# Windowed attention with fp16 copies of fp32 inputs: transposing q and k as 4-byte words, scores from every second fp16, value products grouped by shared weights

## The chip, the cores and the metric

The kernel runs on one core of one Trainium2 chip. Times are device microseconds (us) of an execution, given as medians over executions. All executions quoted here were fast: none was over 1.5% above the fastest of its kernel.

## The reference

Attention inside windows of 64 rows, over 4 x 4096 rows of 1536 numbers:

```python
B, S, D, W = 4, 4096, 1536, 64
logits = np.einsum('bnwd,bnud->bnwu', q_w, k_w) * D ** -0.5
logits = logits - logits.max(axis=-1, keepdims=True)
attn = np.exp(logits); attn = attn / attn.sum(axis=-1, keepdims=True)
out = np.einsum('bnwu,bnud->bnwd', attn, v_w)      # float32 in, float32 out
```

Three inputs of 100.66 MB are read and one output of 100.66 MB is written, so 402.6 MB must cross between HBM and the core, whatever the compute does.

## The kernel before

Work is cut into 32 units of 512 rows. A unit's q, k and v are loaded by GpSimd's software queue, which turns fp32 into fp16 on the way. q and k must be transposed, so that the 1536 columns lie across the partitions. TensorE does that into PSUM, and VectorE (DVE) and ScalarE (ACT) copy the result to SBUF. Score products, the exponential and the value products follow, and the evictions scale by the reciprocal of the row sum. The last unit is cut into three parts to shorten the end.

```python
DC = D // P                       # 12 chunks of 128 columns
tp_ps = ... bufs=3 ...            # PSUM banks for transposes
lt_ps = ... bufs=2 ...            # scores
o_ps  = ... bufs=2 ...            # outputs
s_ps  = ... bufs=1 ...            # row sums
# ... cut ...
def transpose(src, xt, c0, copy):
    tp = tp_ps.tile([P, CG * R, H, P], FP16, tag="tp", name="tp")       # CG = 2 in a full unit
    for c in range(c0, c0 + CG):
        for r in range(R):
            for j in range(H):
                nc.tensor.transpose(tp[:, (c - c0) * R + r, j, :],
                                    src[:, lo + R * j + r, c * P : (c + 1) * P], ident)
    dst = xt[:, c0 : c0 + CG, :].rearrange("p c (r e j) -> p (c r) j e", r=R, j=H)
    copy(out=dst, in_=tp)
# ... cut: product() accumulates the scores; all of q is transposed first, then
#     k group by group, each group followed by the product of the group before it ...
def values(u, i, h, et, last):
    # ... cut: all row sums, then one reciprocal ...
    for t in range(R):
        for j in range(NJ):
            o = o_ps.tile([P, 512], FP32, tag="o", name="o")
            for r in range(R):
                nc.tensor.matmul(o, lhsT=et[:, r, t, :], rhs=u.v[:, lo + R * h + r, sl],
                                 start=(r == 0), stop=(r == R - 1))
            # scaled eviction, in turn on ACT and DVE
# ... cut ...
for ui, u in enumerate(units):
    for i in range(len(u.parts)):
        blocks = scores(u, i)
        if i == 0:
            load_all(ui + 2, "qk")          # q and k have two buffers
        for h, et in blocks:
            values(u, i, h, et, last)
        if not last:
            store(u, i)
    load_all(ui + 3, "v")                   # v has three
```

The softmax here doesn't subtract the row's maximum and nothing guards it: scores larger than these inputs give would overflow.

Of the kernel before, what the change touches and what calls it, by code (L numbers as in the profile page):

```python
# [7 lines left out]
FP16 = mybir.dt.float16  # L8
FP32 = mybir.dt.float32

P = 128
W = 64
EXP = mybir.ActivationFunctionType.Exp
COPY = mybir.ActivationFunctionType.Copy
# [18 lines left out]
def kernel(  # L33
# [6 lines left out]
):  # L40
    nc = tc.nc
    B, S, D = q.shape
    DC = D // P
    NJ = D // 512
    scale = float(D) ** -0.5

# [6 lines left out]
    consts = ctx.enter_context(tc.tile_pool(name="consts", bufs=1))  # L53
    qkp = ctx.enter_context(tc.tile_pool(name="qkp", bufs=2))
    vp = ctx.enter_context(tc.tile_pool(name="vp", bufs=3))
    xtp = ctx.enter_context(tc.tile_pool(name="xtp", bufs=1))
    outp = ctx.enter_context(tc.tile_pool(name="outp", bufs=3))
    rsp = ctx.enter_context(tc.tile_pool(name="rsp", bufs=4))
    tp_ps = ctx.enter_context(tc.tile_pool(name="tp_ps", bufs=3, space=bass.MemoryType.PSUM))
    lt_ps = ctx.enter_context(tc.tile_pool(name="lt_ps", bufs=2, space=bass.MemoryType.PSUM))  # L60
    o_ps = ctx.enter_context(tc.tile_pool(name="o_ps", bufs=2, space=bass.MemoryType.PSUM))
    s_ps = ctx.enter_context(tc.tile_pool(name="s_ps", bufs=1, space=bass.MemoryType.PSUM))

    ctx.enter_context(tc.manual_schedule())
# [17 lines left out]
    def load_all(ui, names):  # L82
# [8 lines left out]
    nc.sync.dma_start(out=slots(raw, 0, SLOTS, SLOTS), in_=rows(qf, 0, SLOTS, SLOTS))  # L91
    load_all(0, "kv")

    ident = consts.tile([P, P], FP16, name="ident")
    ones = consts.tile([P, 8], FP16, name="ones")
    zeros = consts.tile([P, 1], FP32, name="zeros")
    nc.vector.memset(ident, 0.0)
# [3 lines left out]
        out=ident,  # L101
        in_=ident,
# [13 lines left out]
    for R in (2, 1):  # L116
        ets[R] = []
        for i in range(2):
            et = consts.tile([P, R, R, P], FP16, name=f"et{R}{i}")
# [5 lines left out]
    def scores(u, i):  # L125


        lo, hi, R = u.parts[i]
        n = hi - lo
        H = n // R  # L130
        CG = {4: 2, 2: 4, 1: 6}[n]
        xq = xtp.tile([P, DC, n * P], FP16, tag="xq", name="xq")
        xk = xtp.tile([P, DC, n * P], FP16, tag="xk", name="xk")
        lts = []
        for h in range(H):
            lt = lt_ps.tile([P, 512], FP32, tag="lt", name="lt")
            lts.append(lt[:, : R * R * P].rearrange("p (r s e) -> p r s e", r=R, s=R))

        def transpose(src, xt, c0, copy):

            tp = tp_ps.tile([P, CG * R, H, P], FP16, tag="tp", name="tp")
            for c in range(c0, c0 + CG):
                for r in range(R):
                    for j in range(H):
                        nc.tensor.transpose(  # L145
                            tp[:, (c - c0) * R + r, j, :],
                            src[:, lo + R * j + r, c * P : (c + 1) * P],
                            ident,
                        )
            dst = xt[:, c0 : c0 + CG, :].rearrange("p c (r e j) -> p (c r) j e", r=R, j=H)  # L150
            copy(out=dst, in_=tp)  # L151

        def product(c0, h):
            for c in range(c0, c0 + CG):
                kc = xk[:, c, :].rearrange("p (r h e) -> p r h e", r=R, h=H)
                qc = xq[:, c, :].rearrange("p (r h e) -> p r h e", r=R, h=H)
                for r in range(R):
                    nc.tensor.matmul(  # L158
                        lts[h][:, r, :, :],
                        lhsT=kc[:, r, h, :],  # L160
                        rhs=qc[:, :, h, :],
                        start=(c == 0 and r == 0),
                        stop=(c == DC - 1),
                        skip_group_check=True,
                    )

        starts = list(range(0, DC, CG))
        for c0 in starts:
            flip[0] += 1
            transpose(getattr(u, "q"), xq, c0, nc.scalar.copy if flip[0] % 3 == 0 else nc.vector.tensor_copy)  # L170
        for g, c0 in enumerate(starts):
            transpose(getattr(u, "k"), xk, c0, nc.scalar.copy if g % 2 == 1 else nc.vector.tensor_copy)
            if g > 0:
                for h in range(H):
                    product(starts[g - 1], h)
        blocks = []
        for h in range(H):
            product(starts[-1], h)
            et = ets[R][turn[R] % 2]
            turn[R] += 1  # L180
            w = W // R
            for a in range(0, P, w):
                s = slice(a, a + w)
                nc.scalar.activation(  # L184
                    et[s, :, :, s], lts[h][s, :, :, s], EXP, bias=zeros[s], scale=scale
                )
            blocks.append((h, et))
        return blocks

    def values(u, i, h, et, last):  # L190
        lo, hi, R = u.parts[i]
        if not hasattr(u, "o"):
            u.o = outp.tile([P, SLOTS, D], FP32, tag="out_sb", name="out_sb")
        sp = s_ps.tile([P, R, 2], FP32, tag="sp", name="sp")
        for t in range(R):
            for r in range(R):
                nc.tensor.matmul(  # L197
                    sp[:, t, 0:1], lhsT=et[:, r, t, :], rhs=ones[:, 0:1],
                    start=(r == 0), stop=(r == R - 1),
                )  # L200
        rs = rsp.tile([P, R], FP32, tag="rs", name="rs")
        nc.vector.reciprocal(out=rs, in_=sp[:, :, 0])  # L202
        n = 0
        for t in range(R):
            for j in range(NJ):
                o = o_ps.tile([P, 512], FP32, tag="o", name="o")
                sl = slice(512 * j, 512 * (j + 1))
                for r in range(R):
                    nc.tensor.matmul(  # L209
                        o, lhsT=et[:, r, t, :], rhs=u.v[:, lo + R * h + r, sl],  # L210
                        start=(r == 0), stop=(r == R - 1),
                    )
                dst = u.o[:, lo + R * h + t, sl]
                if n % 2 == 0:
                    nc.scalar.activation(dst, o, COPY, bias=0.0, scale=rs[:, t : t + 1])  # L215
                else:
                    nc.vector.tensor_scalar_mul(dst, o, scalar1=rs[:, t : t + 1])  # L217
                n += 1
                if last:
                    nc.sync.dma_start(out=of[u.first[i] : u.first[i] + P, sl], in_=dst)  # L220
# [5 lines left out]
    for ui, u in enumerate(units):  # L226
        for i in range(len(u.parts)):
            last = ui == N - 1 and i == len(u.parts) - 1
            blocks = scores(u, i)
            if i == 0:  # L230
                load_all(ui + 2, "qk")
# [4 lines that stand above are left out]
        load_all(ui + 3, "v")  # L236
# [30 lines left out]
```

## Time and profile before

| | before |
|---|---|
| time | 950.44 us, median of 3 (949.48 to 950.64) |
| traffic | 402.6 MB, 424 GB/s |
| distance between units in mid-run | 29.5 us |
| TensorE waiting for k in a unit | 2.8 us on average (78.4 us in 28 waits) |

First, lines of the page of the kernel before: the span; busy time of each engine with its instructions; the DMA row (busy tenths of the 16 DMA engines in each of 40 slices); the packet time of the main queue as a share of 16 engines' span; the HBM traffic.

```profile
span 948.6 us, 12985 instructions
...
PE 666.8 (70%) x5624; PEld 443.1 (47%) x5624; DVE 426.9 (45%) x491; ACT 434.2 (46%) x612; POOL 83.7 (9%) x139
...
DMA  9999999999999999999999999999999999999997
...
q0 software_dynamic: 27232, 249.31, 100.2%
...
HBM read 301.99 MB, written 100.66 MB: 424 GB/s over the span
```

The DMA row reads 9 in 39 of 40 slices, while the busiest engine, TensorE, is busy for 70%. "HBM Reference" of the Trainium skill, under Specifications (TRN2), gives about 425 GB/s for a core that streams alone; this trace has 424. (The prediction below names the section Access; the figure stands under Specifications.)

Next, groups of instructions of the same page: line, engine, operation, shapes, count | busy us, mean ns of one | idle time before them and what ended most of it.

```profile
...
L209 PE MATMUL o<-v,et 128*128 128x512 f16 x762 | 226.8, 402 | 65.6 <-ACT out_sb L215 61.4
L158 PE MATMUL lt<-xq,xk 128*128 128x256 f16 (+1 forms) x1536 | 236.9, 306 | 41.4 <-DVE xk L151 25.9
L151 ACT COPY xk<-tp 128x1024 f16<-128x1024 f16 (+1 forms) x96 | 123.6, 1287 | 255.8 <-PE tp L145 255.8
...
L151 DVE COPY xk<-tp 128x1024 f16<-128x1024 f16 (+1 forms) x97 | 123.3, 1271 | 200.7 <-PE tp L145 200.7
...
L145 PE MATMUL tp<-ident,k 128*128 128x128 f16 x1536 | 136.4, 245 | 81.7 <-DMA k<-in_k_dram 78.4
...
L209 PEld LDWEIGHTS <-et 128*128 128x128 f16 x762 | 72.7, 99 | 188.1 <-issue 147.5
...
L145 PE MATMUL tp<-ident,q 128*128 128x128 f16 x1536 | 103.0, 220 | 46.6 <-DVE xq L151 20.8
```

A PSUM copy takes 1.27 to 1.29 us. The value products (L209) have as many weight loads as matmuls. A transpose's mean of 220 or 245 ns is how long one takes from its start to its end. In a burst they overlap, and the timeline gives the real rate.

The waits view of the kernel before: who waited for whom, us in total, number of waits, longest.

```profile
...
PE tp L145 <- DMA k<-in_k_dram: 78.4, 28, 4.3
...
PE tp L145 <- DMA q<-in_q_dram: 3.2, 4, 1.4
```

And TensorE's timeline over one unit (start us, length us, what, count [idle before, releaser]):

```profile
...
330.54 1.50 PE L145 MATMUL tp<-ident,q 128*128 128x128 f16 x24
...
337.20 1.07 PE L145 MATMUL tp<-ident,k 128*128 128x128 f16 x16 [2.67 <-DMA k<-in_k_dram]
339.27 1.89 PE L158 MATMUL lt<-xq,xk 128*128 128x256 f16 x8 [1.01 <-DVE xk L151]
...
346.87 0.61 PE L145 MATMUL tp<-ident,k 128*128 128x128 f16 x8
347.55 1.05 PE L158 MATMUL lt<-xq,xk 128*128 128x256 f16 x8
...
359.99 1.50 PE L145 MATMUL tp<-ident,q 128*128 128x128 f16 x24
```

This unit starts at 330.54 and the next at 359.99. The q transposes come first, then a wait of 2.67 us for k. Eight k transposes take 0.61 us later on, which is 77 ns each with the latency of the burst counted in. 24 q transposes take 1.50 us. Eight score matmuls take 1.05 us at the end of the stage. "TensorE: Matmul & The Clock Gate" of the Trainium skill (Part 1) describes a clock that falls to half when the engine has been idle. This trace agrees: here is the stretch behind the wait (us; busy us of PE, PEld, DVE, ACT, POOL; granted clock; DMA share; GB/s), with a granted clock of 0.50.

```profile
...
338.20:344.95 6.75, 5.74 (x37) 4.58 (x36) 2.32 (x2) 1.63 (x2) 0.00 (x0) 0.50 1.02 293
```

The 16 transposes right behind the wait still ran at the full rate (1.07 us); the clock fell a microsecond later.

Last, the end of the run, in stretches of the trace (us; busy us of each engine; granted clock; DMA share; GB/s):

```profile
...
930.00:935.00 5.00, 4.34 (x39) 2.56 (x38) 2.89 (x5) 1.53 (x3) 0.55 (x1) 0.79 0.79 337
935.00:940.00 5.00, 3.13 (x40) 2.14 (x37) 1.94 (x4) 3.03 (x6) 0.55 (x1) 1.00 0.82 347
940.00:949.00 9.00, 1.51 (x10) 0.57 (x10) 0.92 (x2) 2.45 (x5) 0.00 (x0) 0.82 0.49 193
```

### The profile page before, as it was taken

Reading aid. Unit: us, or ns where it says so; the run is one execution under the profiler, and the core shown is the slowest. Engines: PE = TensorE matmul, PEld = TensorE weight load, DVE = VectorE, ACT = ScalarE, POOL = GpSimd, SP = SyncE. Lnnn points to the kernel's source line nnn. Section 1 sums busy time; section 2 is a strip of 40 time slices with the busy share of each in tenths; the row PEclk is TensorE's granted clock in tenths of the full one; section 3 lists DMA queues with packets and bytes.
Section 4 is the critical chain, followed back from the end, with each engine's and each line's share of the span. In section 5 each row is a group of like instructions: output and inputs, shape, how many; then the busy total and the mean of one; then the engine's idle time right before and its main releaser. Section 6 shows DMA issues by size and latency. Waiting matters only on the chain. (4 is left out here: it accounts for less than half of the span.)

```text
span 948.6 us, 12985 instructions
## 1 busy us (share of the span) xinstructions
PE 666.8 (70%) x5624; PEld 443.1 (47%) x5624; DVE 426.9 (45%) x491; ACT 434.2 (46%) x612; POOL 83.7 (9%) x139
## 2 busy tenths in 40 slices
PE   2777776776767867767667677776776767777685
PEld 1544554444544545445454354544445534455452
DVE  3545445443454344543445443454434545344442
ACT  2555434444345444454534454435544445453444
POOL 1101110100101011010010100101101001011010
PEclk9999989888899889798988998989988999798798
DMA  9999999999999999999999999999999999999997
GB/s 259 215 234 262 282 280 280 247 253 279 281 278 252 246 282 282 279 263 242 278 281 279 271 241 271 282 279 275 242 263 282 281 277 253 254 279 281 279 258 312
DMA packets 27865, 254.07 MB, mean 268 GB/s; under 512 B 2208, under 2 KB 2208, under 8 KB 11808
## 3 DMA queue, kind: packets, MB, share of 16 engines
q0 software_dynamic: 27232, 249.31, 100.2%
q1 hardware_dynamic: 576, 3.93, 1.1%
q8 instruction: 44, 0.72, 0.3%
q14 instruction: 13, 0.11, 0.0%
HBM read 301.99 MB, written 100.66 MB: 424 GB/s over the span
## 5 line engine op out<-in xcount | busy, mean ns | idle before, releaser
L209 PE MATMUL o<-v,et 128*128 128x512 f16 x762 | 226.8, 402 | 65.6 <-ACT out_sb L215 61.4
L158 PE MATMUL lt<-xq,xk 128*128 128x256 f16 (+1 forms) x1536 | 236.9, 306 | 41.4 <-DVE xk L151 25.9
L151 ACT COPY xk<-tp 128x1024 f16<-128x1024 f16 (+1 forms) x96 | 123.6, 1287 | 255.8 <-PE tp L145 255.8
L217 DVE TENSOR_SCALAR out_sb<-o,rs 128x512 f32<-128x512 f32 x191 | 143.4, 751 | 161.7 <-PE o L209 161.7
L151 DVE COPY xk<-tp 128x1024 f16<-128x1024 f16 (+1 forms) x97 | 123.3, 1271 | 200.7 <-PE tp L145 200.7
L158 PEld LDWEIGHTS <-xk 128*128 128x128 f16 x1536 | 154.1, 110 | 92.3 <-DVE xk L151 39.0
L145 PE MATMUL tp<-ident,k 128*128 128x128 f16 x1536 | 136.4, 245 | 81.7 <-DMA k<-in_k_dram 78.4
L215 ACT ACTIVATE out_sb<-o,rs 128x512 f32<-128x512 f32 x193 | 132.7, 687 | 123.4 <-PE o L209 112.2
L145 PEld LDWEIGHTS <-k 128*128 128x128 f16 x1536 | 118.1, 112 | 94.1 <-DMA k<-in_k_dram 83.2
L209 PEld LDWEIGHTS <-et 128*128 128x128 f16 x762 | 72.7, 99 | 188.1 <-issue 147.5
L151 DVE COPY xq<-tp 128x1024 f16<-128x1024 f16 (+1 forms) x129 | 152.1, 1255 | 5.1 <-PE tp L145 5.0
L145 PE MATMUL tp<-ident,q 128*128 128x128 f16 x1536 | 103.0, 220 | 46.6 <-DVE xq L151 20.8
L145 PEld LDWEIGHTS <-q 128*128 128x128 f16 x1536 | 91.9, 98 | 64.6 <-issue 34.8
L151 ACT COPY xq<-tp 128x1024 f16<-128x1024 f16 x64 | 82.1, 1283 | 83.7 <-PE tp L145 83.7
L184 ACT ACTIVATE et<-lt,zeros 32x128 f16<-32x128 f32 (+1 forms) x256 | 91.8, 359 | 32.9 <-PE lt L158 27.4
L202 DVE RECIPROCAL rs<-sp 128x2 f32<-128x2 f32 (+1 forms) x65 | 10.7, 165 | 133.7 <-PE sp L197 133.7
L224 POOL DMA_DIRECT2D out_dram<-out_sb x33 | 23.2, 704 | 419.0 <-issue 376.6
L80 POOL DMA_DIRECT2D k<-in_k_dram x34 | 18.5, 546 | 352.1 <-PE tp L145 210.4
L197 PE MATMUL sp<-ones,et 128*128 128x1 f16 x254 | 16.0, 166 | 41.1 <-ACT et L184 41.1
L197 PEld LDWEIGHTS <-et 128*128 128x128 f16 x254 | 13.6, 98 | 60.0 <-ACT et L184 50.4
L80 POOL DMA_DIRECT2D q<-in_q_dram x33 | 17.9, 542 | 79.1 <-PE tp L145 58.8
L80 POOL DMA_DIRECT2D v<-in_v_dram x34 | 23.9, 703 | 4.9 <-DMA k<-in_k_dram 4.9
(12 smaller groups left out, 7.6 us busy)
## 6 DMA issues: line engine op xcount, KB each, us to landing
out_dram<-out_sb POOLq DMA_DIRECT2D x31, 3072.0 KB, 41.9
k<-in_k_dram POOLq DMA_DIRECT2D x31, 1536.0 KB, 48.6
v<-in_v_dram POOLq DMA_DIRECT2D x31, 1536.0 KB, 48.7
q<-in_q_dram POOLq DMA_DIRECT2D x30, 1536.0 KB, 53.8
raw<-in_q_dram SPq DMA_DIRECT2D x1, 3072.0 KB, 14.5
out_dram<-out_sb POOLq DMA_DIRECT2D x1, 1536.0 KB, 10.0
v<-in_v_dram POOLq DMA_DIRECT2D x1, 768.0 KB, 46.9
v<-in_v_dram POOLq DMA_DIRECT2D x2, 384.0 KB, 46.4
```

The lines of the kernel that those rows point to most:

```text
L80: nc.gpsimd.dma_start(out=dst, in_=rows(src, u.first[i], hi - lo, r))
L145: nc.tensor.transpose(tp[:, (c - c0) * R + r, j, :], src[:, lo + R * j + r, c * P : (c + 1) * P], ident,)
L151: copy(out=dst, in_=tp)
L158: nc.tensor.matmul(lts[h][:, r, :, :], lhsT=kc[:, r, h, :], rhs=qc[:, :, h, :], start=(c == 0 and r == 0), stop=(c == DC - 1), skip_group_ ...
L184: nc.scalar.activation(et[s, :, :, s], lts[h][s, :, :, s], EXP, bias=zeros[s], scale=scale)
L197: nc.tensor.matmul(sp[:, t, 0:1], lhsT=et[:, r, t, :], rhs=ones[:, 0:1], start=(r == 0), stop=(r == R - 1),)
L202: nc.vector.reciprocal(out=rs, in_=sp[:, :, 0])
L209: nc.tensor.matmul(o, lhsT=et[:, r, t, :], rhs=u.v[:, lo + R * h + r, sl], start=(r == 0), stop=(r == R - 1),)
L215: nc.scalar.activation(dst, o, COPY, bias=0.0, scale=rs[:, t : t + 1])
L217: nc.vector.tensor_scalar_mul(dst, o, scalar1=rs[:, t : t + 1])
L224: nc.gpsimd.dma_start(out=rows(of, u.first[i], hi - lo, R), in_=slots(u.o, lo, hi, R))
```

## The change

The intent was to shorten three things. Two neighbouring fp16 numbers are transposed together as one 4-byte word, so there are half as many transposes, and the PSUM copies have half as many elements. The score products then take every second fp16 of the result. The value products are reordered so that those with the same weights follow one another, together with the row sum. For that, one PSUM bank moves from the transposes to the outputs.

```diff
-    DC = D // P
+    DC = D // (2 * P)
-    tp_ps = ... bufs=3      o_ps = ... bufs=2
+    tp_ps = ... bufs=2      o_ps = ... bufs=3
-    ident = consts.tile([P, P], FP16, name="ident")
+    ident = consts.tile([P, P], FP32, name="ident")
# ... cut: FP32 tiles xq, xk, tp; half the chunks in a group ...
+                        pairs = src[:, lo + R * j + r, :].bitcast(FP32)
                         nc.tensor.transpose(
-                            tp[:, (c - c0) * R + r, j, :], src[:, lo + R * j + r, c * P : (c + 1) * P], ident,
+                            tp[:, (c - c0) * R + r, j, :], pairs[:, c * P : (c + 1) * P], ident
                         )
# ... cut: product(); kc and qc are the fp16 view of a chunk, with an index w for the half ...
+                for w in range(2):
+                            lhsT=kc[:, r, h, :, w], rhs=qc[:, :, h, :, w],
# values():
         for t in range(R):
+            os = [o_ps.tile([P, 512], FP32, tag="o", name="o") for j in range(NJ)]
+            for r in range(R):
+                w = et[:, r, t, :]
+                nc.tensor.matmul(sp[:, t, 0:1], lhsT=w, rhs=ones[:, 0:1], start=first, stop=done)
+                for j in range(NJ):
+                    nc.tensor.matmul(os[j], lhsT=w, rhs=..., start=first, stop=done)
+            nc.vector.reciprocal(out=rs[:, t : t + 1], in_=sp[:, t, 0:1])
             for j in range(NJ):
# ... cut: three scaled evictions ...
```

More of the change, by code (lines that the diff above doesn't have):

```diff
@@ L58 @@
     rsp = ctx.enter_context(tc.tile_pool(name="rsp", bufs=4))
-    tp_ps = ctx.enter_context(tc.tile_pool(name="tp_ps", bufs=3, space=bass.MemoryType.PSUM))
+    tp_ps = ctx.enter_context(tc.tile_pool(name="tp_ps", bufs=2, space=bass.MemoryType.PSUM))
     lt_ps = ctx.enter_context(tc.tile_pool(name="lt_ps", bufs=2, space=bass.MemoryType.PSUM))
-    o_ps = ctx.enter_context(tc.tile_pool(name="o_ps", bufs=2, space=bass.MemoryType.PSUM))
+    o_ps = ctx.enter_context(tc.tile_pool(name="o_ps", bufs=3, space=bass.MemoryType.PSUM))
     s_ps = ctx.enter_context(tc.tile_pool(name="s_ps", bufs=1, space=bass.MemoryType.PSUM))
@@ L130, in scores @@
         H = n // R
-        CG = {4: 2, 2: 4, 1: 6}[n]
-        xq = xtp.tile([P, DC, n * P], FP16, tag="xq", name="xq")
-        xk = xtp.tile([P, DC, n * P], FP16, tag="xk", name="xk")
+        CG = {4: 1, 2: 2, 1: 3}[n]
+        xq = xtp.tile([P, DC, n * P], FP32, tag="xq", name="xq")
+        xk = xtp.tile([P, DC, n * P], FP32, tag="xk", name="xk")
         lts = []
@@ L139, in transpose @@
         def transpose(src, xt, c0, copy):
-            tp = tp_ps.tile([P, CG * R, H, P], FP16, tag="tp", name="tp")
+            tp = tp_ps.tile([P, CG * R, H, P], FP32, tag="tp", name="tp")
             for c in range(c0, c0 + CG):
@@ L144, in transpose @@
                     for j in range(H):
+                        pairs = src[:, lo + R * j + r, :].bitcast(FP32)
                         nc.tensor.transpose(
-                            tp[:, (c - c0) * R + r, j, :],
-                            src[:, lo + R * j + r, c * P : (c + 1) * P],
-                            ident,
+                            tp[:, (c - c0) * R + r, j, :], pairs[:, c * P : (c + 1) * P], ident
                         )
@@ L151, in transpose, with halves @@
             copy(out=dst, in_=tp)
+        def halves(xt, c):
+            return xt[:, c, :].bitcast(FP16).rearrange("p (r h e w) -> p r h e w", r=R, h=H, w=2)
         def product(c0, h):
             for c in range(c0, c0 + CG):
-                kc = xk[:, c, :].rearrange("p (r h e) -> p r h e", r=R, h=H)
-                qc = xq[:, c, :].rearrange("p (r h e) -> p r h e", r=R, h=H)
-                for r in range(R):
-                    nc.tensor.matmul(
-                        lts[h][:, r, :, :],
-                        lhsT=kc[:, r, h, :],
-                        rhs=qc[:, :, h, :],
-                        start=(c == 0 and r == 0),
-                        stop=(c == DC - 1),
-                        skip_group_check=True,
-                    )
+                kc, qc = halves(xk, c), halves(xq, c)
+                for w in range(2):
+                    for r in range(R):
+                        nc.tensor.matmul(
+                            lts[h][:, r, :, :],
+                            lhsT=kc[:, r, h, :, w],
+                            rhs=qc[:, :, h, :, w],
+                            start=(c == 0 and w == 0 and r == 0),
+                            stop=(c == DC - 1 and w == 1),
+                            skip_group_check=True,
+                        )
         starts = list(range(0, DC, CG))
@@ L194, in values @@
         sp = s_ps.tile([P, R, 2], FP32, tag="sp", name="sp")
-        for t in range(R):
-            for r in range(R):
-                nc.tensor.matmul(
-                    sp[:, t, 0:1], lhsT=et[:, r, t, :], rhs=ones[:, 0:1],
-                    start=(r == 0), stop=(r == R - 1),
-                )
         rs = rsp.tile([P, R], FP32, tag="rs", name="rs")
-        nc.vector.reciprocal(out=rs, in_=sp[:, :, 0])
         n = 0
         for t in range(R):
+            os = [o_ps.tile([P, 512], FP32, tag="o", name="o") for j in range(NJ)]
+            for r in range(R):
+                first, done = r == 0, r == R - 1
+                w = et[:, r, t, :]
+                nc.tensor.matmul(sp[:, t, 0:1], lhsT=w, rhs=ones[:, 0:1], start=first, stop=done)
+                for j in range(NJ):
+                    nc.tensor.matmul(
+                        os[j], lhsT=w, rhs=u.v[:, lo + R * h + r, 512 * j : 512 * (j + 1)],
+                        start=first, stop=done,
+                    )
+            nc.vector.reciprocal(out=rs[:, t : t + 1], in_=sp[:, t, 0:1])
             for j in range(NJ):
-                o = o_ps.tile([P, 512], FP32, tag="o", name="o")
                 sl = slice(512 * j, 512 * (j + 1))
-                for r in range(R):
-                    nc.tensor.matmul(
-                        o, lhsT=et[:, r, t, :], rhs=u.v[:, lo + R * h + r, sl],
-                        start=(r == 0), stop=(r == R - 1),
-                    )
                 dst = u.o[:, lo + R * h + t, sl]
                 if n % 2 == 0:
-                    nc.scalar.activation(dst, o, COPY, bias=0.0, scale=rs[:, t : t + 1])
+                    nc.scalar.activation(dst, os[j], COPY, bias=0.0, scale=rs[:, t : t + 1])
                 else:
-                    nc.vector.tensor_scalar_mul(dst, o, scalar1=rs[:, t : t + 1])
+                    nc.vector.tensor_scalar_mul(dst, os[j], scalar1=rs[:, t : t + 1])
                 n += 1
```

## The prediction

> **What bounds the kernel now.** The transfers. The page has the DMA engines at 9 tenths or more in 39 of 40 slices, the software queue's packets fill 100.2% of 16 engines' span, and HBM traffic (302 MB read, 101 MB written) runs at 424 GB/s. That is what a core streaming alone gets by the Trainium skill ("HBM Reference", Access: about 425 GB/s); this trace agrees. The change touches no transfer.
>
> Compute is next, and close. One unit of 512 rows takes 29.5 us (timeline, distance between stores in mid-run). In it TensorE waits about 2.7 us for k to land (waits view: 78.4 us in 28 waits). So compute needs about 26.8 us, a slack near 9%.
>
> **What the change does, per unit.**
> - Transposes: 96 fp16 ones become 48 four-byte ones. A burst of 8 now takes 0.61 us (77 ns each, 7.4 us per unit). I assume one pass each: the Trainium skill ("TensorE: Matmul & The Clock Gate", Terms) says that the transpose mode is four times faster for FP32, and (Weight-path perf modes) that FP32 gets no fast weight load. No trace here shows it yet. Estimate from that page's 128 columns / 1.2 GHz: about 110 ns each, 5.3 us; saves 2 us.
> - Copies out of PSUM: 12 of 128x1024 fp16 (1.26 us DVE, 1.28 us ACT) become 12 of 128x512 words. Scaling an output of 512 fp32 takes 0.75 (DVE) and 0.69 us (ACT), so about 0.7: some 6.5 us of engine time less, on the chain about 2 us in the q stage (paced by four DVE copies, 4.8 us) and 1 to 3 in the k stage.
> - Scores: 48 matmuls as before, 130 ns each in bursts, operands now every second fp16. I expect little change.
> - Values: matmuls and weight loads on this line are equal in number (762) although the last parts already reuse weights in a row, so grouping removes no weight load. Three banks now finish together and are evicted while TensorE waits. Estimate 2.4 us per group, four groups, 9.6 us against 8.8 now: costs 1 us.
>
> **Sum.** Compute falls from 26.8 to about 23 us, but that only lengthens the wait for k to 5 or 6 us; DMA still sets 29.5. On the critical path lie only the last two units, which in the timeline don't wait for loads; DMA shares there (0.81 and 0.49 in the last two 10 us stretches) leave some 6 us of idle DMA, of which I expect 2 to 3.
>
> **Predicted:** 947 us, 8 in 10 between 940 and 962. Faster by over 2%: 0.03; within 2%: 0.84; slower: 0.13.
>
> **What would show it.** Right: the DMA row still at 9s and about 424 GB/s; wait for k near 5 us per unit; half as many transposes, one pass each; copies near 0.7 us; weight loads of the value line equal to its matmuls; DVE and ACT each 90 to 110 us less busy. Wrong: transposes over 200 ns in a burst; score matmuls well over 130 ns; DMA row below 9.
>
> **What would make it wrong.** Four passes per four-byte transpose: 48 at about 430 ns, +13 us per unit, about 1,300 us. Strided operands at half rate: +5 us per unit, compute back at the DMA's period, the same time or a few per cent over. Two passes and slow strides together: 33 us per unit, 1,050 us. A result faster by over 2% would mean that DMA was not at its limit.

## The result and the profile after

| | before | after |
|---|---|---|
| time, median of 4 | 949.96 us | 947.21 us (946.87 to 947.76) |
| ratio of fast runs | | 0.9972, 95% interval 0.9954 to 0.9989 |
| instructions on TensorE | 5624 matmuls | 4088 |
| DVE busy, ACT busy | 426.9, 434.2 us | 315.2, 318.6 us |

A ratio is always the mean time of one kernel's fast runs over that of the other's in the same rounds, so it is not quite the ratio of the medians quoted beside it. By the 2% rule the verdict is "same", with a small gain that is outside the noise.

The same lines of the page, after:

```profile
span 945.3 us, 10170 instructions
...
PE 662.5 (70%) x4088; PEld 449.4 (48%) x4088; DVE 315.2 (33%) x554; ACT 318.6 (34%) x612; POOL 83.7 (9%) x139
...
DMA  9999999999999999999999999999999999999997
...
q0 software_dynamic: 27232, 249.31, 100.3%
...
HBM read 301.99 MB, written 100.66 MB: 426 GB/s over the span
```

The DMA row has not changed. The groups that answer to those shown of before:

```profile
...
L207 PE MATMUL o<-v,et 128*128 128x512 f16 x762 | 202.3, 377 | 50.6 <-ACT out_sb L216 34.2
L161 PE MATMUL lt<-xq,xk 128*128 128x256 f16 (+1 forms) x1536 | 225.7, 298 | 6.4 <-DVE xk L151 6.3
L147 PE MATMUL tp<-ident,q 128*128 128x128 f32 x768 | 142.6, 340 | 101.7 <-DMA q<-in_q_dram 70.7
L147 PE MATMUL tp<-ident,k 128*128 128x128 f32 x768 | 133.3, 312 | 72.3 <-DMA k<-in_k_dram 70.5
...
L151 ACT COPY xk<-tp 128x512 f32<-128x512 f32 (+1 forms) x96 | 58.6, 610 | 275.2 <-PE tp L147 275.2
L151 DVE COPY xk<-tp 128x512 f32<-128x512 f32 (+1 forms) x97 | 66.9, 690 | 246.5 <-PE tp L147 246.5
...
L207 PEld LDWEIGHTS <-et 128*128 128x128 f16 x762 | 62.0, 96 | 112.8 <-issue 60.0
```

There are half as many transposes. Each copy takes 0.61 us on ACT and 0.69 on DVE. Weight loads of the value line still equal its matmuls, 762 and 762, so grouping removed none. The waits:

```profile
...
PE tp L147 <- DMA q<-in_q_dram: 70.7, 28, 3.8
PE tp L147 <- DMA k<-in_k_dram: 70.5, 30, 3.2
```

TensorE now waits 141.2 us for loads, against 81.6 before. What compute saved turned into waiting, and all of the increase is for q; the wait for k itself fell from 78.4 to 70.5 us. One unit of the timeline:

```profile
...
335.24 1.83 PE L147 MATMUL tp<-ident,k 128*128 128x128 f32 x8 [3.11 <-DMA k<-in_k_dram]
337.07 1.87 PE L161 MATMUL lt<-xq,xk 128*128 128x256 f16 x8
...
342.81 0.60 PE L147 MATMUL tp<-ident,k 128*128 128x128 f32 x4
343.24 1.98 PE L161 MATMUL lt<-xq,xk 128*128 128x256 f16 x16
...
348.68 0.95 PE L207 MATMUL o<-v,et 128*128 128x512 f16 x3 [0.72 <-ACT out_sb L216]
...
357.12 1.06 PE L147 MATMUL tp<-ident,q 128*128 128x128 f32 x8 [2.66 <-DMA q<-in_q_dram]
```

Four 4-byte transposes take 0.60 us, a single one 0.27, so about 110 ns for each further one ((0.60 - 0.27) / 3). That is twice the 56 ns of an fp16 one ((1.50 - 0.61) / 16). A group of four takes as long as the group of eight that it replaces (0.61 us), so TensorE's own time for transposes has not fallen. From the start of one score matmul to the next there are 113 ns at stride 2 and 109 at stride 1 (medians of the start times in the two traces). The end of the run:

```profile
...
930.00:935.00 5.00, 2.58 (x22) 1.56 (x22) 1.67 (x4) 2.56 (x6) 0.54 (x1) 1.00 0.99 420
935.00:940.00 5.00, 0.00 (x0) 0.00 (x0) 0.00 (x0) 0.00 (x0) 0.00 (x0) 0.61 0.80 326
940.00:949.00 9.00, 0.00 (x0) 0.00 (x0) 0.00 (x0) 0.00 (x0) 0.00 (x0) 0.59 0.11 44
```

Compute now stops at 934.9 us; after that only transfers run, and the span ends at 945.3. Before, compute worked until 944.1.

### The profile page after: what moved, and what is told of

The parts are those of the page before. It is cut to its first block, busy times and chain, and to the rows that moved or that the text cites. A ratio compares the mean times of both kernels' runs of the same rounds, so it can differ in the third digit from the quotient of the medians.

```text
span 945.3 us, 10170 instructions
## 1 busy us (share of the span) xinstructions
PE 662.5 (70%) x4088; PEld 449.4 (48%) x4088; DVE 315.2 (33%) x554; ACT 318.6 (34%) x612; POOL 83.7 (9%) x139
## 3 DMA queue, kind: packets, MB, share of 16 engines
q0 software_dynamic: 27232, 249.31, 100.3%
## 5 line engine op out<-in xcount | busy, mean ns | idle before, releaser
L207 PE MATMUL o<-v,et 128*128 128x512 f16 x762 | 202.3, 377 | 50.6 <-ACT out_sb L216 34.2
L147 PE MATMUL tp<-ident,q 128*128 128x128 f32 x768 | 142.6, 340 | 101.7 <-DMA q<-in_q_dram 70.7
L147 PE MATMUL tp<-ident,k 128*128 128x128 f32 x768 | 133.3, 312 | 72.3 <-DMA k<-in_k_dram 70.5
L147 PEld LDWEIGHTS tp<-ident,q 128*128 128x128 f32 x768 | 107.5, 173 | 143.3 <-issue 101.1
L151 ACT COPY xk<-tp 128x512 f32<-128x512 f32 (+1 forms) x96 | 58.6, 610 | 275.2 <-PE tp L147 275.2
L151 DVE COPY xk<-tp 128x512 f32<-128x512 f32 (+1 forms) x97 | 66.9, 690 | 246.5 <-PE tp L147 246.5
L147 PEld LDWEIGHTS tp<-ident,k 128*128 128x128 f32 x768 | 106.4, 162 | 84.2 <-issue 77.0
L151 DVE COPY xq<-tp 128x512 f32<-128x512 f32 (+1 forms) x129 | 86.7, 687 | 107.1 <-PE tp L147 104.2
L151 ACT COPY xq<-tp 128x512 f32<-128x512 f32 x64 | 39.0, 609 | 189.3 <-PE tp L147 189.3
L205 PE MATMUL sp<-ones,et 128*128 128x1 f16 x254 | 42.4, 167 | 40.6 <-ACT et L187 40.6
```

What stands on the lines that cost most here:

```text
L147: nc.tensor.transpose(tp[:, (c - c0) * R + r, j, :], pairs[:, c * P : (c + 1) * P], ident)
L205: nc.tensor.matmul(sp[:, t, 0:1], lhsT=w, rhs=ones[:, 0:1], start=first, stop=done)
L207: nc.tensor.matmul(os[j], lhsT=w, rhs=u.v[:, lo + R * h + r, 512 * j : 512 * (j + 1)], start=first, stop=done,)
```

## The experiments

Twelve kernels ran. In the "resident" ones the loads after the first buffers are taken away, and all units reuse these buffers. Their outputs are wrong, which doesn't matter for the times. They measure compute with its stores. The complete kernels all passed the check of their results.

```diff
     def load(u, i, name):
+        ui = u.row0 // UR
+        keep = 3 if name == "v" else 2
+        if ui >= keep:
+            setattr(u, name, getattr(units[ui % keep], name))
+            return
```

### Compute alone, before and after

The edit is the one above, made in each of the two kernels.

> The kernel before, with loads only for the first two units of q and k and three of v; later units reuse those buffers, so the result is wrong on purpose and the time is that of compute plus stores. Theory (transfers set the period, compute hides under them): the compute period of 26.8 us read from the trace, less what a warmer TensorE clock gives, so 32 units plus some 20 us of start and end: 790 to 875 us. Rival (the wait for k is only an artefact and compute itself sets the 29.5 us): 930 us or more.

> The changed kernel with the same loads taken away. Theory: 60 to 80 us below the same experiment on the kernel before (2 to 2.5 us per unit, 32 units), so about 720 to 810 us. Rival (faster copies and slower transposes or evictions cancel, so the change saves no compute): within 15 us of the same experiment on the kernel before.

They took 842.14 us (2 executions) and 751.72 us (2). Compute fits well under the transfers in both kernels, and the change removes 90 us of it, which is more than I had expected. So the change does what it was meant to do. It does so off the critical path.

TensorE's timeline of the resident kernel before also shows the first score burst of a unit:

```profile
...
409.63 1.05 PE L163 MATMUL lt<-xq,xk 128*128 128x256 f16 x8 [0.92 <-DVE xk L156]
```

With no wait for a load ahead of it, it runs in 1.05 us, not 1.89. The mean granted clock is 0.966, against 0.901 in the full kernel. So without the waits for loads the clock is low less often, and part of the slack of the full kernel was hidden in its low clock.

### Transfers alone

Compute is taken out; loads, stores, sizes, buffers and queues stay, except that the last part of the output goes through GpSimd's queue like the rest (the hardware queue has 144 packets in place of 576). A one-column read of every loaded slot keeps the order of events.

```diff
-        blocks = scores(u, i)
+        for name in "qk": touch(u, i, name)           # copies one column of each slot
         if i == 0: load_all(ui + 2, "qk")
-        for h, et in blocks: values(u, i, h, et, last)
+        touch(u, i, "v")
+        for s in range(lo, hi): nc.scalar.copy(out=u.o[:, s, :], in_=u.v[:, s, :])
         store(u, i)
```

> The same loads and stores, sizes, buffers and queues as in the changed kernel, with nearly all compute taken out (a one-column read of every loaded slot, and a copy of v into the output tile, so the result is wrong on purpose). Theory (the transfer rate is the floor): 935 to 948 us, no more than 1% below the changed kernel. Rival (the transfers wait for compute to free buffers or to issue them): below 925 us.

It took 946.42 us (ratio 0.9963 to the kernel before; interval 0.9948 to 0.9977). Its page:

```profile
span 944.5 us, 954 instructions
...
DMA  9999999999999999999999999999999999999997
...
q0 software_dynamic: 27376, 250.09, 100.5%
...
HBM read 301.99 MB, written 100.66 MB: 426 GB/s over the span
```

This is the floor of these transfers in this order. A kernel that computes next to nothing is 0.1% faster than the changed one (0.9963 against 0.9972, intervals overlapping), and only 0.4% faster than the kernel before. It is no floor for every order of transfers: here too the DMA engines are idle for some 7 us at the end (19.5 us from 925 us on, less 24 x a share of 0.52 in that stretch).

### Adding compute on purpose

Useless 512-column matmuls go ahead of each k transpose group of a full unit. The transposes then overwrite what they wrote, so the results stay right.

```diff
             tp = tp_ps.tile(...)
+            if n == 4 and xt is xk:
+                for _ in range(3):        # 6 in the other pair
+                    nc.tensor.matmul(tp_as_512_fp32, lhsT=src[:, lo, 0:P], rhs=src[:, lo, 0:512], start=True, stop=True)
```

> The kernel before with 18 useless matmuls of 512 columns per unit (3.9 us at full clock). Its compute alone took 25.65 us per unit, so 29.55 us with them against 29.5 us of transfers: theory says 950 to 975 us. Rival (compute far from the limit): 948 to 951 us as if nothing were added.

> The changed kernel with the same 3.9 us. Its compute alone took 22.7 us per unit, so 26.6 us with them: theory says no change at all within 0.3%, 946 to 950 us, apart from up to 3 us at the end. Rival (the period hangs on the latency of compute through buffers and issues, not on the rate of the transfers): a rise by more than 10 us.

> The kernel before with six useless matmuls of 512 columns (about 216 ns each at full clock) ahead of each of the six k transpose groups of a full unit, 7.8 us per unit; the result stays right. Theory: slack is 2.7 us of waiting plus up to 2.3 us that come back as a warmer clock, so the time rises by 2.8 to 5.1 us per unit, to 1,035 to 1,110 us. Rival (a large reserve in compute): below 970 us.

> The changed kernel with the same 36 useless matmuls per unit. Theory: its slack is 4.7 us of waiting plus the same clock effect, so it rises by 0 to 3.1 us per unit, to 947 to 1,045 us, and stays at least 50 us below the same experiment on the kernel before. Rival (the change saved no compute): both rise alike.

| added per unit (nominal) | before | after |
|---|---|---|
| 0 | 950.0 | 947.2 |
| 3.9 us | 948.8 (0.9988; 0.9972 to 1.0005) | 949.5 (0.9994; 0.9979 to 1.0008) |
| 7.8 us | 1028.5 (1.0824; 1.0792 to 1.0855) | 973.8 (1.0248; 1.0218 to 1.0278) |

3.9 us per unit are about 120 us in all (31 x 3.9), and neither kernel became slower than the kernel before. The changed one is 0.2% above its own 947.2, as was expected of it. I had given the kernel before a rise of 0 to 25 us; it had none, and so lies where the rival had put it: its reserve in compute is larger than my sum said. Its waits view says where part of the room was:

```profile
...
PE tp L144 <- DMA k<-in_k_dram: 26.8, 18, 2.8
```

It still waits for k, though 26.8 us in all rather than 78.4, and its mean clock is 0.957 rather than 0.901. With 7.8 us both kernels break through the floor, and in neither does TensorE wait for loads of q or k any more. The one before rises by 78 us, the changed one by 27. So the change is worth some 50 us as soon as compute is what limits. Both stay below the sum of compute alone and 31 x 7.8 us: the changed one by 20 us, the kernel before by 55 us and therefore just under the 1,035 to 1,110 us that I had expected. Part of the added work went into waits for copies: TensorE waits 57 us for copies of q and k there, and 84 us in the resident kernel before.

### Which part of the change saves the compute

Resident runs with one part each: first the transposes with the stride-2 scores, keeping three transpose banks and the old value part; then the regrouped values with two transpose banks and fp16 transposes.

```diff
 # transposes alone, starting from the changed kernel
-    tp_ps bufs=2, o_ps bufs=3, values() as changed
+    tp_ps bufs=3, o_ps bufs=2, values() as before
 # values alone, starting from the kernel before
-    tp_ps bufs=3, o_ps bufs=2, values() as before
+    tp_ps bufs=2, o_ps bufs=3, values() as changed
```

> Loads taken away as in the first two experiments; of the change only the four-byte transposes and the stride-2 scores, with the kernel before's value part and its split of PSUM (3 banks for transposes, 2 for outputs). In the resident pair the q stage took 4.57 us before and 4.75 after, the k and score stage 11.73 and 10.09. Theory: the transposes give about 1.5 to 2 us per unit, 842 down to 780 to 795 us. Rival (all of the gain comes from the value part): 835 us or more.

> Loads taken away; of the change only the regrouped value products with its split of PSUM (2 banks for transposes, 3 for outputs); fp16 transposes as before. The prediction had said that this part costs 1 us per unit (870 us here); the resident pair shows the value stage 1.4 us shorter (9.34 to 7.89), which would give about 795 to 810 us; but the third transpose bank is gone and may take back up to 1 us per unit, so 795 to 840 us.

Both expectations missed. The transposes alone take 742.46 us, less than the whole change (751.72). The values alone take 894.32 us, 52 us *more* than the kernel before. Cutting TensorE's timeline into stages explains it (from the first q transpose to the first k transpose, to the first row sum, to the next unit; means of 22 to 27 units, us; resident kernels):

| resident kernel | transpose banks | q stage | k and scores | values | unit | mean clock |
|---|---|---|---|---|---|---|
| before | 3 | 4.57 | 11.73 | 9.34 | 25.65 | 0.966 |
| whole change | 2 | 4.75 | 10.09 | 7.89 | 22.72 | 0.999 |
| transposes alone | 3 | 3.19 | 10.04 | 9.13 | 22.36 | 0.977 |
| values alone | 2 | 6.99 | 12.41 | 7.88 | 27.28 | 0.900 |

The gain in the k and score stage comes with the shorter copies. TensorE's own time there is as before (0.60 us for four transposes, 0.61 for eight), but its score products wait less for a copy of k. These waits are, in the resident kernel before (for DVE's copies; 9.0 us more for ACT's) and in the one with the whole change (for DVE's, none for ACT's):

```profile
...
PE lt L163 <- DVE xk L156: 28.4, 32, 1.0
...
PE lt L166 <- DVE xk L156: 9.8, 33, 0.4
```

Regrouping makes the value stage 1.2 to 1.5 us shorter with either kind of transpose. A quarter to a third of that is the clock: in the resident kernel before, the stage takes 8.84 us in the 12 units where its clock was full and 9.80 us in the 12 where it was 0.82 or 0.83; regrouped at full clock it takes 7.88. Together with the bank that it takes from the transposes, regrouping costs 1.6 us in the q stage with the short copies (4.75 against 3.19) and 2.4 us with the long ones (6.99 against 4.57). In the values-alone kernel one sees the bursts of q transposes broken up by waits for a copy, and run at a low clock (eight in 1.01 us; 0.61 before):

```profile
...
404.80 1.01 PE L150 MATMUL tp<-ident,q 128*128 128x128 f16 x8 [0.23 <-DVE xq L156]
```

In the resident kernel with the whole change, TensorE waits this long for DVE's q copies:

```profile
...
PE tp L152 <- DVE xq L156: 32.2, 62, 1.2
```

And in that with the transposes alone:

```profile
...
PE tp L152 <- DVE xq L156: 0.3, 1, 0.3
```

The stages point to the bank. No run changed the number of banks and nothing else, so that is read from the stages, not isolated. A rival is that regrouping lets three evictions end together just when the q stage begins, so that DVE starts its copies late. The traces give it a small part: the first q copy starts 1.15 us after the first q transpose in both regrouped kernels and 0.87 in the two others, a delay of 0.3 us.

To see whether it is the load on DVE (four of six q copies) rather than the bank, the q copies of the resident changed kernel were shared evenly:

```diff
-            ... nc.scalar.copy if flip[0] % 3 == 0 else nc.vector.tensor_copy
+            ... nc.scalar.copy if flip[0] % 2 == 0 else nc.vector.tensor_copy
```

> The changed kernel without loads, with the q copies shared evenly by VectorE and ScalarE in place of two to one. The prediction expected the shorter copies to shorten the q stage by 2 us; it stayed at 4.75 us. If the run of copies on VectorE (four of six) with two transpose banks still paces the stage, it falls to 3.5 to 4.2 us and the time by 15 to 40 us; if TensorE's own 24 transposes of 110 ns and their latency pace it, the time stays within 8 us of 752.

749.25 us, and the q stage at 4.68 us, against 751.72 and 4.75. The share of DVE was not it. Nor is it TensorE's own 24 transposes, the other cause that I had named, although the time fell in the range given for it: the transposes alone do the same 24 in a q stage of 3.19 us.

### Looking for a faster version

Two tries in the full kernel. First, the transposes alone with all loads in place, since their compute is the shortest:

> The complete kernel, all loads in place, with only the transpose part of the change (three transpose banks and two output banks, and the value part, as in the kernel before). Its compute alone is 9 us less than that of the whole change. Theory (transfer rate): nothing of that shows, 945 to 949 us, the ratio to the kernel before between 0.995 and 0.999. If compute still mattered inside the run: 2 us or more below the whole change's 0.9972, so a ratio under 0.995.

947.27 us, ratio 0.9972 (0.9958 to 0.9985): the same as the whole change. The 9 us of compute that it saves against it are invisible, as the transfer floor demands.

Second, stores issued from SyncE's hardware queue, so that loads don't queue behind a store that waits for its last eviction:

```diff
-        nc.gpsimd.dma_start(out=rows(of, ...), in_=slots(u.o, lo, hi, R))
+        nc.sync.dma_start(out=rows(of, ...), in_=slots(u.o, lo, hi, R))
```

> The changed kernel with its stores issued from SyncE in place of GpSimd, so that loads no longer queue behind a store that waits for the last eviction. Theory (transfer rate): 940 to 950 us, within 0.7% of the changed kernel. Rival (the order and moment of issue limit the transfers): below 935 us.

953.56 us, ratio 1.0036 (1.0021 to 1.0051), 0.6% above the changed kernel and just outside what theory had said. The queue lines of its page:

```profile
...
q0 software_dynamic: 18512, 149.43, 74.9%
q1 hardware_dynamic: 9296, 103.81, 26.4%
```

"DMA: Bandwidth & Descriptors" of the Trainium skill (Issuing engines are not separate DMA queues) says that DMAs from all queues end up on the same 16 engines, so that spreading them saves only issue time. This run agrees that nothing is gained, and the split even cost a little: the two shares together are 101.3% of a span that is 7 us longer, for the same bytes. Why the split costs 0.6% is open. No version was found that is clearly faster than the changed kernel, and the run without compute leaves 0.1% to be found in compute. Other sizes or another order of the transfers at the end were not tried.

## Why the prediction was right, point by point

- **DMA sets the time: right, and shown.** Transfers alone need 946.4 us; compute alone needs 842 and then 752. The wait for loads grew from 81.6 to 141.2 us. Predicted was a wait of 5 to 6 us per unit for k; it is 4.6 us (141.2 / 31 full units), half for q and half for k. The sign that the prediction had named, a longer wait for k, did not come: 2.3 us per unit, a little less than before.
- **Time: 947 predicted, 947.21 measured.** That the two agree to 0.2 us is luck, because where the 2.7 us come from was mostly wrong: I put 2 to 3 us into idle DMA at the end. The profiled spans differ by 3.3 us (948.6 and 945.3). By the last stretches of the trace (from 930 us to the end of the span, less shares times lengths), idle DMA there fell only from 6.1 to 5.4 us. The rest lies in the transfers themselves, as far as one profiled execution of each tells: the packet times of the whole trace, added up and divided by 16 engines, are 963.4 us before and 960.7 after (packets overlap, so the sum is above the span). Of these 2.7 us, 0.7 are less fetching of instructions (44 packets on that queue, then 32), and 1.75 are the main queue: the same 27,232 packets, 0.2% quicker. Why they are quicker is open.
- **Transposes: rate right, saving wrong.** They take 110 ns each in a burst, as estimated. The saving of 2 us was a slip: it set 77 ns, with the latency of the burst counted in, against 110 ns without. Like for like, 96 x 56 ns became 48 x 110 ns, about 5.3 us both times. Whether 110 ns at full granted clock is one pass, as assumed, no run shows.
- **Copies: right in size, wrong on the chain.** They take 0.61 and 0.69 us, and DVE and ACT are 112 and 116 us less busy (90 to 110 predicted). In the k and score stage they give most of the 1.6 us (11.73 to 10.09) that the prediction had put at 1 to 3. The step "on the chain about 2 us in the q stage" failed for the whole change: with compute alone the stage went from 4.57 to 4.75 us. With three banks and the old value part it falls to 3.19, so the gain was there and, as far as the stages tell, the lost bank took it back. I had read the changed bank numbers in the diff and given them no term.
- **Scores: right.** Eight take 1.07 us at stride 2, against 1.05 at stride 1. "SBUF — State Buffer" of the Trainium skill (Specifications) asks for two or more hits in each 16-byte line for full bandwidth; stride 2 gives four, and the loss is 4 ns per matmul (113 against 109, start to start), whose cause no run isolates.
- **Values: wrong sign.** I had 9.6 us against 8.8, a cost of 1. Measured with compute alone: 7.89 against 9.34, a gain of 1.4, of which about 0.5 is the clock. A group of three takes 2.1 us, not 2.4: in the unit shown, the groups' first products start at 346.47, 348.68, 350.75 and 352.84. TensorE starts the next group as soon as the first of the three banks is free (0.72 us of idle at 348.68), so filling and evicting overlap more than I had counted. That no weight load would go was right.
- **Compute period: 26.8 to 23 predicted, 25.65 to 22.72 measured.** Reading the period as distance minus wait was 1.1 us too high. The low clock behind the wait fits this: the 6.75 us at a clock of 0.50 in the unit shown.

So the sum for compute came close by luck: two gains that were not there (2 us in the transposes, 2 us in the q stage) stand against a cost of 1 us in the values that was a gain of 1.4. Hidden under the transfers, none of these errors could reach the total.

## What to carry to other kernels

When the DMA row is full, time the transfers alone before improving compute: one such run would have said that, with these transfers, at most 0.4% was to be had. Compare rates like for like: a burst of eight divided by eight still holds its latency, and that alone made a saving of 2 us out of nothing. Waiting time on TensorE understated the slack here, because work behind a wait ran at a granted clock of 0.50: 3.9 us more per unit fitted where the waits showed 2.8. A change that moves a PSUM bank should be costed for the stage that loses the bank as well as for the one that gains it, and its parts tried apart: here one part alone had the shorter compute.

## What the Trainium skill lacked or had wrong

- "TensorE: Matmul & The Clock Gate", Part 4 (PE-mode transpose), has about 275 ns for a 128x128 bf16 transpose in a kernel and none for 4-byte words. In bursts, from start to start at full granted clock, the runs show 56 ns for fp16 and about 110 ns for a 4-byte word.
- The same page's advice against idle gaps of more than about 3 us between matmul bursts is not strict enough where transposes lie around the gap: after a wait of 2.67 us behind q transposes, the granted clock was 0.50 and eight score matmuls took 1.89 us in place of 1.05. Its remark in Part 4 that transposes do not count as busy in the same way would fit, but the clock also stayed at 1.00 while TensorE ran nothing but transposes, with short waits, from 402.71 to 409.63 us of the resident kernel before. No run here isolates it.
- "DMA: Bandwidth & Descriptors" (Issuing engines are not separate DMA queues) does not say that splitting loads and stores between the software and a hardware queue can cost: 953.56 us against 947.21.
